# Softmax probabilities of a latent attention transposed by VectorE and DMAs through DRAM instead of TensorE, with the row sums applied to the gate

## The chip, the cores and the metric

The kernel runs on one core of one Trainium2 chip, in a single launch. The metric is the device time of the launch in microseconds. Three runs of the kernel before gave a median of 770.55 us (770.55 to 770.92).

## The reference

A trunk of two layers works on 512 tokens of width 1024, with 16 learned meta tokens ahead of them (528 tokens in all). Everything is float32. Each layer runs two token mixers on the same normalized input and adds their gated sum to the residual stream; the meta positions are dropped at the end. Cut to what matters:

```python
h = rmsnorm(h_res, norm_gain[l])
proj = h @ w_in[l]
u_pool, z_pool, c_q, c_kv, k_rope, z_mla, g_pool, g_mla = split(proj)
y_pool = (pool_mix(u_pool, ...) * silu(z_pool)) @ pool_w_up[l]
o_mla = mla(c_q, c_kv, k_rope, pos, ...)            # 8 heads, 96 wide for q and k, 64 for v
y_mla = (o_mla * silu(z_mla)) @ mla_w_up[l]
merged = sigmoid(g_pool) * y_pool + sigmoid(g_mla) * y_mla
h_res = h_res + merged @ w_out[l]
```

The attention inside `mla`, for each head, with a causal mask:

```python
s = einsum('bqhd,bkhd->bhqk', q, k) * scale
p = softmax(where(valid, s, MASK_VALUE), axis=-1)
o = einsum('bhqk,bkhd->bqhd', p, v)
```

## The kernel before

Activations lie transposed in SBUF, features on the partitions and the 528 tokens along the free dimension. Every float32 product is made of three passes of TensorE in a faster float32 format: an operand is split in a high part (a ScalarE copy) and a low part (a VectorE subtraction), and `mm3` (lines 180 to 184, the lines L181, L182 and L183 of the profile) multiplies high by high, high by low and low by high. Weights come by DMA on SP's queue into raw buffers (`fetch`, L114), and `wload` splits each 128x512 piece into `whi` (ScalarE, L176) and `wlo` (VectorE, L177), three buffers each, four pieces ahead.

The order of the program is written by hand. All weight products stand in one list `plan`; `stream` walks through it, and each `step` issues the next few matmuls and adds their planned duration (n columns at 2.4 GHz) to a clock. Attention and the norms are written as ordinary code that pulls filler from this stream: `fill_now(ns)` issues so much of it, and `gap` issues `FILL` ns but stops when the product named by `RESERVE` is done, so that later ones are left over for the end of the attention. The filler of the attention of a layer is, in this order, `pu0` to `pu7` (the end of the pooling mixer), `zm0` to `zm3`, `gp0` to `gp7` and `gm0` to `gm7` (the gates). `after(ns, fn)` issues something so much planned time later, and the tile scheduler orders the instructions of each engine by its own timeline; `follow` and `behind` add dependencies to it. Layer 1 leaves out the meta queries.

One head of the attention has these steps. `prep` scales the keys of the head (VectorE L742, GpSimd L743), splits them into `kh` and `kl`, splits the queries and copies their rotary part by SBUF-to-SBUF DMA (L756). `head` makes the scores of four blocks of 128 queries against their causal keys (272, 400, 528 and 144 columns, the 528 in two parts, L771 and L806), adds the mask and takes the row maximum on VectorE (L774), and exponentiates on ScalarE with the row sum as accumulator (L781) into the tiles `pa`, `pb` and `pc`. VectorE inverts the sums (L827), and GpSimd multiplies the probabilities by them (L834, and L832 for the 16 meta columns). `pv` of the previous head transposes the ten causal 128x128 blocks through TensorE against an identity (L859), splits each result out of PSUM into `th` and `tl` (ScalarE L275, VectorE L276), and multiplies by V: `both` (L872) takes the high part against V's high and low halves, `low` (L876) the low part against V's high half. It is cut in three parts that lie around the gaps of the next head, and some of its passes are interleaved with other matmuls (`hosts`). The 16 meta columns of two heads are collected in `pm`, transposed in four 32x128 pieces (L848), split (L903 to L905) and multiplied at once (L922). The result is multiplied by `silu(z_mla)`, which lies in `zms`.

There are four gaps a head, eight heads a layer.

Of the kernel before, what the change touches and what calls it, by code (L numbers as in the profile page):

```python
# [18 lines left out]
P = 128  # L19
DEPTH = 2  # L20
# [32 lines left out]
FILL = (2950.0, 2850.0)  # L53
RESERVE = ("gm5", "gm5")
# [3 lines left out]
WARM = 8  # L58

# [12 lines left out]
def trunk(ctx, tc, xT, xrow, mrow, pos, win, wkr, wqb, wkb, wvb, wgr, wpu, wmu, wout, gains, const, yT):  # L72
# [23 lines left out]
    def sqt():  # L96
        return tp.tile([P, HALF], F32, tag="sq", name=nm("sq"), bufs=16)
# [72 lines left out]
    def wload(src, n, spare):  # L170
        raw = early.pop(0) if early else fetch(src, n, rawt(), sp)
        loads[0] += 1
        pool, th, tl, nb = (tp, "th", "tl", 2) if loads[0] <= 2 or spare else (wp, "whi", "wlo", 3)
        hi = pool.tile([P, W if pool is tp else 512], F32R, tag=th, name=nm("whi"), bufs=nb)
        lo = pool.tile([P, W if pool is tp else 512], F32R, tag=tl, name=nm("wlo"), bufs=nb)
        act.activation(hi[:, :n], raw[:, :n], AF.Copy)  # L176
        dve.tensor_sub(lo[:, :n], raw[:, :n], hi[:, :n].bitcast(F32))  # L177
        return hi, lo
# [134 lines left out]
    kdr = [dp.tile([H, T], F32, name=f"kdr{l}") for l in range(DEPTH)]  # L313

    hbuf = [(slot(f"hh{k}", F32R), slot(f"hl{k}", F32R)) for k in range(8)]

    class Layer:
        def __init__(self, l):
# [11 lines left out]
            self.sq = []  # L330
# [147 lines left out]
        def kr_rest(self, a, b):  # L478
# [5 lines left out]
            q = sqt()  # L484
# [82 lines left out]
        def mix(self, m, s):  # L567
# [7 lines left out]
            t = "tl" if m % 2 else "th"  # L575
            self.ys[m] = (slot(f"u{m}", F32R), tp.tile([P, W], F32R, tag=t, name=nm(t), bufs=2))
# [46 lines left out]
        def ev_k(self, p):  # L623
            def ev(ps, a, b):
# [6 lines left out]
                q = self.ksq[:, a:b] if p < 3 else sqt()[:, :b - a]  # L631
# [5 lines left out]
        def v_body(self, k, w):  # L637
# [17 lines left out]
            ps = mmt()  # L655
            for k in range(2):
                r = slot("pa", F32R, bufs=2, w=416)[:, 0:4 * NM].rearrange("p (a b) -> p a b", a=4)
# [18 lines left out]
        def q_stat(self, ps, a, b, c):  # L676
            for a0, b0 in FULL:
                a0, b0 = max(a, a0), min(b, b0)
                if a0 < b0:
                    q = sqt()  # L680
                    made = act.activation(q[:, :b0 - a0], ps[:, a0 - a:b0 - a], AF.Square)
                    self.stat(q[:, :b0 - a0], a0, b0, c, made)
# [76 lines left out]
        def head(self, h, kq, prev):  # L759
# [3 lines left out]
            pa = slot("pa", bufs=2, w=416)  # L763
            pb = slot(f"cq{8 + odd}")
            pc = slot(f"cq{10 + odd}")
            bia = sm.tile([P, 5], F32, tag="bia", name=nm("bia"), bufs=2)
            rs = sm.tile([P, 5], F32, tag="rs", name=nm("rs"), bufs=2)

# [17 lines left out]
            first = scores(1, s1, 0, 272)  # L786
            if self.hosted is not None:
                follow(first, self.hosted)
            scores(3, s3, 0, SPL)
            tops = [top(1, 1, s1, causal(272)), top(3, 4, s3, maskw[:, 0:SPL])]  # L790
# [3 lines left out]
            self.tops = tops + [top(2, 2, s2, causal(400))]  # L794
# [9 lines left out]
            scores(3, s4, SPL, T)  # L804
            def passes(out, q0, n):
# [3 lines left out]
            if self.last:  # L809
                scores(0, s0, 0, 144)  # L810
            else:
                sm_ = sc[0:NM, 432:432 + NM]
                todo = passes(s0, slice(NM, NM + P), 144) + passes(sm_, slice(0, NM), NM)
                if prev is None:
                    for fn in todo:
                        fn()
                else:
                    self.pv(prev, 1, todo)
# [6 lines left out]
            expo(0, 0, s0, pt[0])  # L825
            dve.tensor_add(rs[:, 3:4], rs[:, 3:4], rs[:, 4:5])
            dve.reciprocal(rs[:, 0:4], rs[:, 0:4])  # L827
            if odd == 0:
                self.pm = sm.tile([P, 4, 32], F32, tag="pm", name=nm("pm"), bufs=2)
            for i in range(4):  # L830
                n = pt[i].shape[1]
                gp.tensor_mul(self.pm[:, i, 16 * odd:16 * odd + 16], pt[i][:, 0:NM],  # L832
                              rs[:, i:i + 1].to_broadcast([P, NM]))
# [3 lines left out]
        def pv(self, prev, part, hosts=()):  # L837
            if prev is None:
                return
            h, pt, pm = prev  # L840
            p, odd = h // 2, h % 2
            final = h == H - 1
            if part == 0:
                self.o = sct() if final else pp.tile([P, 512], F32, tag="o", name=nm("o"), bufs=1)
                if odd == 1:
                    self.turn = srows[:, 0:512].rearrange("p (c i r) -> p c i r", c=4, i=4)
                    for c in range(4):
                        ins = dve.transpose(self.turn[:, c].rearrange("p a b -> p (a b)"),  # L848
                                            pm[32 * c:32 * c + 32].rearrange("p a b -> p (a b)"))
                        if not final:  # L850
                            for t in self.tops:
                                follow(ins, t)
            ops = self.o

            def turned(js):
                tr, c = mmt(), 0
                for j in js:
                    for i in range(j, 4):
                        pe.transpose(tr[:, c:c + P], pt[i][:, NM + P * j:NM + P * (j + 1)], ident)  # L859
                        c += P  # L860
                th = tp.tile([P, W], F32R, tag="th", name=nm("th"), bufs=2)
                tl = tp.tile([P, W], F32R, tag="tl", name=nm("tl"), bufs=2)
                return th, tl, split(th, tl, tr[:, :c], 0, c)

            def ready(t, fn):
                ins = fn()
                behind(ins, t[2])
                return ins

            def both(j, t, c):  # L870
                n = SEQ - P * j
                return pe.matmul(ops[:, P * j:512], vt[:, j, h, :], t[0][:, c:c + n], start=j == 0, stop=j == 3)  # L872

            def low(j, t, c, a=0, b=512):
                a, b = max(a, P * j), min(b, 512)
                return pe.matmul(ops[0:64, a:b], vt[:, j, h, 0:64], t[1][:, c + a - P * j:c + b - P * j],  # L876
                                 start=False, stop=j == 3, skip_group_check=True)

            def chain(*fns):
                last = None  # L880
                for fn in fns:
                    ins = fn()
                    if last is not None:
                        follow(ins, last)
                    last = ins
                return last

            if part == 0:
                self.t01 = [turned((0,)), turned((1,))]
            if part == (0 if final else 1):  # L890
                t0, t1 = self.t01
                if hosts:
                    chain(lambda: both(0, t0, 0), lambda: ready(t0, hosts[0]), lambda: low(0, t0, 0, 0, 256), hosts[1],
# [323 lines left out]
```

## Time and profile before

| | |
|---|---|
| median of three runs | 770.55 us |
| span of the profiled execution (its own time is not listed apart from its span) | 768.5 us |
| TensorE, weight loads (PEld) | 763.8 us (99%), 697.9 us (91%) |
| VectorE, ScalarE, GpSimd | 544.1 us (71%), 408.9 us (53%), 201.6 us (26%) |
| DMA | 84.05 MB, 35.6% of 16 engines on SP's queue |
| L859, transposes through TensorE | 160 instructions |
| L834, L832 on GpSimd | 64 and 64 instructions |

A profile is of one execution. A busy time is the time in which at least one instruction of the engine ran; matmuls overlap, so the duration of one (mean ns) is longer than its place in the stream. In rows of groups the shapes are out<-in, then come the count, the busy time, the mean and the idle time of the engine ahead of them with what ended it. In the list of waits a row reads: engine, tile and line, what it waited for, total us, times, longest us.

### The profile page before, as it was taken

What the parts mean: (1) busy time and instruction counts of PE and PEld (TensorE: products, weight loads), DVE (VectorE), ACT (ScalarE), POOL (GpSimd) and SP (SyncE); (2) the same over time, 40 slices, a digit from 0 to 9 for tenths busy, and PEclk for the clock granted to TensorE, in tenths of its full rate; (3) what the DMA queues carried; (4) which work ended last, traced back from release to release, by engine and by line L of the source; (5) the groups of instructions that cost most, each with busy time, mean ns of one, the idle gap of its engine ahead of it and who ended that gap; (6) DMA issues with size and microseconds to landing.
All of it is one profiled execution on the core that took longest, in us unless ns stands there. A gap on an engine that the chain in (4) does not pass through costs nothing.

```text
span 768.5 us, 14355 instructions
## 1 busy us (share of the span) xinstructions
PE 763.8 (99%) x5195; PEld 697.9 (91%) x5195; DVE 544.1 (71%) x1179; ACT 408.9 (53%) x892; POOL 201.6 (26%) x251
## 2 busy tenths in 40 slices
PE   9999999999999999999999999999999999999998
PEld 9999999999999999999997898887888888888887
DVE  5588687357899977785376486773677989775842
ACT  6755656545556665634264355454446666664320
POOL 2026204012242233052220262040132434420500
PEclk9999999999999999999999999999999999999999
DMA  8533233343223222325642333334433332222372
GB/s 293 160 113 98 75 97 98 104 141 105 89 79 91 84 71 70 107 71 169 178 133 97 110 86 89 96 87 127 125 119 90 94 93 77 82 69 70 119 222 98
DMA packets 54931, 84.05 MB, mean 109 GB/s; under 512 B 10006, under 2 KB 18582, under 8 KB 54860
## 3 DMA queue, kind: packets, MB, share of 16 engines
q1 hardware_dynamic: 54716, 82.87, 35.6%
q8 instruction: 41, 0.67, 0.4%
q14 instruction: 30, 0.25, 0.1%
q10 hardware_dynamic: 144, 0.26, 0.1%
HBM read 76.69 MB, written 4.29 MB: 105 GB/s over the span
## 4 chain that ended last, share of the span: by engine, by line
PE 99%; DMA 0%; ACT 0%; DVE 0%; SPq 0%; issue 0%; ACTq 0%
PE mm L181 29%; PE mm L183 29%; PE mm L182 29%; PE mm L859 2%; PE S L181 2%; PE S L182 2%; PE S L183 2%; PE o L876 1%; PE o L872 1%; PE S L503 1%; PE S L470 0%; DMA xb<-xT 0%; PE S L806 0%; PE mm L922 0%; PE mm L395 0%; PE S L872 0%
## 5 line engine op out<-in xcount | busy, mean ns | idle before, releaser
L181 PE MATMUL mm<-hh,whi 128*128 128x264 f32 (+2 forms) x1080 | 339.9, 317 | 0.0
L182 PE MATMUL mm<-hl,whi 128*128 128x264 f32 (+2 forms) x1080 | 338.2, 314 | 0.0
L183 PE MATMUL mm<-hh,wlo 128*128 128x264 f32 (+2 forms) x1080 | 337.1, 315 | 0.0
L177 DVE TENSOR_TENSOR wlo<-raw,whi 128x512 fp32r<-128x512 f32 (+2 forms) x251 | 186.7, 748 | 98.6 <-ACT whi L176 94.6
L176 ACT ACTIVATE whi<-raw 128x512 fp32r<-128x512 f32 (+2 forms) x251 | 150.2, 602 | 181.3 <-PE mm L182 135.3
L181 PEld LDWEIGHTS mm<-hh,whi 128*128 128x128 f32 x1080 | 202.5, 188 | 12.9 <-ACT kp L474 0.4
L182 PEld LDWEIGHTS mm<-hl,whi 128*128 128x128 f32 x1080 | 203.0, 188 | 12.2
L183 PEld LDWEIGHTS mm<-hh,wlo 128*128 128x128 f32 x1080 | 201.9, 188 | 12.2
L743 POOL TENSOR_TENSOR tmp<-kp,bc 64x528 f32<-64x528 f32 x16 | 25.6, 1600 | 123.9 <-PE mm L183 70.0
L604 POOL TENSOR_TENSOR racc<-racc,tmp 128x264 f32<-128x264 f32 (+1 forms) x15 | 14.3, 956 | 133.1 <-ACT tmp L603 133.1
L832 POOL TENSOR_TENSOR pm<-pa,rs 128x16 f32<-128x16 f32 x32 | 9.1, 285 | 126.1 <-DVE rs L827 126.1
L982 POOL TENSOR_TENSOR tmp<-tmp,xb 128x264 f32<-128x264 f32 (+1 forms) x24 | 26.9, 1138 | 56.0 <-DVE tmp L980 55.9
L774 DVE CUSTOM_DVE_ANT_0 S<-S,maskw,nqs 128x400 f32<-128x400 f32 (+4 forms) x80 | 38.4, 499 | 4.4 <-PE S L183 4.0
L781 ACT ACTIVATE cq<-S,bia 128x400 f32<-128x400 f32 (+2 forms) x48 | 24.6, 516 | 27.1 <-DVE bia L774 18.1
L181 PE MATMUL mm<-u,whi 128*128 128x264 f32 (+1 forms) x108 | 34.7, 322 | 0.0
L181 PE MATMUL mm<-cq,whi 128*128 128x264 f32 (+1 forms) x108 | 34.7, 321 | 0.0
L183 PE MATMUL mm<-u,wlo 128*128 128x264 f32 (+1 forms) x108 | 34.7, 321 | 0.0
L183 PE MATMUL mm<-cq,wlo 128*128 128x264 f32 (+1 forms) x108 | 34.5, 321 | 0.0
L182 PE MATMUL mm<-cq,whi 128*128 128x264 f32 (+1 forms) x108 | 34.5, 321 | 0.0
L834 POOL TENSOR_TENSOR cq<-cq,rs 128x384 f32<-128x384 f32 (+1 forms) x32 | 32.8, 1024 | 0.0
L276 DVE TENSOR_TENSOR tl<-mm,th 128x384 fp32r<-128x384 f32 (+1 forms) x48 | 27.9, 596 | 5.0 <-ACT th L275 4.8
L275 ACT ACTIVATE th<-mm 128x384 fp32r<-128x384 f32 (+1 forms) x48 | 24.1, 523 | 10.2 <-PE mm L859 9.2
(270 smaller groups left out, 1378.6 us busy)
## 6 DMA issues: line engine op xcount, KB each, us to landing
raw<-win SPq DMA_DIRECT2D x143, 256.0 KB, 2.6
raw<-wout SPq DMA_DIRECT2D x32, 256.0 KB, 3.0
bc<-kdr SPq DMA_DIRECT2D x16, 264.0 KB, 3.6
raw<-wpu SPq DMA_DIRECT2D x16, 256.0 KB, 2.7
raw<-wmu SPq DMA_DIRECT2D x16, 256.0 KB, 2.7
raw<-wqb SPq DMA_DIRECT2D x12, 256.0 KB, 2.6
xb<-xT SPq DMA_DIRECT2D x8, 264.0 KB, 5.7
tmp<-xT SPq DMA_DIRECT2D x16, 132.0 KB, 3.4
```

Of the source, the lines that this page charges most:

```text
L176: act.activation(hi[:, :n], raw[:, :n], AF.Copy)
L177: dve.tensor_sub(lo[:, :n], raw[:, :n], hi[:, :n].bitcast(F32))
L181: first = pe.matmul(out, wh, xh, start=start, stop=False)
L182: pe.matmul(out, wh, xl, start=False, stop=False)
L183: newest[0] = pe.matmul(out, wl, xh, start=False, stop=stop)
L275: act.activation(hi[:, a:b], src, AF.Copy)
L276: return dve.tensor_sub(lo[:, a:b], src, hi[:, a:b].bitcast(F32))
L743: gp.tensor_mul(kf[r0:r0 + 64, :], self.kp[r0:r0 + 64, :], bc[r0:r0 + 64, :])]
L774: return dve.tensor_tensor_reduce(out=sv, in0=sv, in1=mask, scale=nqs[:, i, h:h + 1], scalar=3e38, op0=ALU.add, op1=ALU.min, accum_out=bia ...
L781: act.activation(pv, sv, AF.Exp, scale=-1.0, bias=bia[:, i:i + 1], accum_out=rs[:, c:c + 1])
L834: gp.tensor_mul(pt[i][:, NM:], pt[i][:, NM:], rs[:, i:i + 1].to_broadcast([P, n - NM]))
L982: gp.tensor_add(t[:, :b - a], t[:, :b - a], self.am[m][:, a:b])
```

## The change

The transposes through TensorE are dropped. When a query block has been exponentiated, the new function `turn` copies its 16 meta columns (GpSimd) and lets VectorE transpose its causal 128x128 blocks in 32x32 pieces into one tile D of ten blocks. After the last block, SP issues four DMAs, one for each 32 partitions, that write D to a DRAM buffer with the 32x32 pieces at their transposed places, and GpSimd issues one DMA that reads it back into a tile E. In the next head, `parts` splits E into high (a `wide` tile) and low (in place), in two pieces of 640 columns, and `pv` multiplies, now in one piece, its moving operand read in runs of 32 columns out of that layout. The probabilities are no longer multiplied by the inverted row sums. Instead these are written to DRAM, read back spread over 64 partitions by a DMA that GpSimd issues, and multiplied into `zms` on GpSimd, once for two heads. The meta columns are transposed in one piece, split, written to DRAM and read back by three DMAs (`meta_turn`).

The fillers shrink, the reserve grows, tile D has one buffer and E two, the second buffers of `pa`, `pb` and `pc` go, and the squares for the norms move from tiles of their own into parts of `xb`, D and E (`halves`). `th` and `tl` become halves of one wide tile.

```diff
-FILL = (2950.0, 2850.0)
-RESERVE = ("gm5", "gm5")
+FILL = (2620.0, 2530.0)
+RESERVE = ("gm3", "gm3")
+NB = 10
+def block(i, j):
+    return 2 * i + j if j < 2 else 1 if i == 2 else 6 + j
...
+    def att(tag):
+        return sl.tile([P, NB * P], F32 if tag == "D" else F32R, tag=f"att{tag}", name=nm(f"att{tag}"), bufs=1 if tag == "D" else 2)
...
+            def turn(i):
+                gp.tensor_copy(pm[:, i, 16 * odd:16 * odd + 16], pt[i][:, 0:NM])
+                for j, n in ((0, i + 1),) if i in (0, 1, 3) else ((0, 2), (2, 1)):
+                    k = block(i, j)
+                    dve.transpose(grid[:, :, k:k + n, :].rearrange("p b s r -> p s b r"), pt[i][:, NM + P * j:NM + P * (j + n)])
...
             expo(1, 1, s1, pt[1])
             expo(2, 2, s2, pt[2])
+            turn(1)
+            turn(2)
             self.gap()
-            self.pv(prev, 0)
-            if self.last:
-                self.pv(prev, 1)
+            self.parts(prev)
             self.gap()
...
             expo(0, 0, s0, pt[0])
+            turn(3)
+            turn(0)
             dve.tensor_add(rs[:, 3:4], rs[:, 3:4], rs[:, 4:5])
             dve.reciprocal(rs[:, 0:4], rs[:, 0:4])
-            for i in range(4):
-                n = pt[i].shape[1]
-                gp.tensor_mul(self.pm[:, i, 16 * odd:16 * odd + 16], pt[i][:, 0:NM],
-                              rs[:, i:i + 1].to_broadcast([P, NM]))
-                gp.tensor_mul(pt[i][:, NM:], pt[i][:, NM:], rs[:, i:i + 1].to_broadcast([P, n - NM]))
-            return h, pt, self.pm
+            row = rdr[self.l][h]
+            sp.dma_start(row.rearrange("a (p i) -> p (a i)", i=4), rs[:, 0:4])
+            got = att("E")
+            n = NB * 32
+            via = pdr[h % 2]
+            for a in range(4):
+                sp.dma_start(via[:, n * a:n * a + n].rearrange("(b k) x -> k b x", k=32),
+                             blocks[32 * a:32 * a + 32, :].rearrange("p (b x) -> p b x", x=n))
+            gp.dma_start(got.bitcast(F32), via)
+            gp.dma_start(rb[64 * odd:64 * odd + 64, 0:512], row.partition_broadcast(64))
+            if odd == 1:
+                self.meta_turn(pm)
+                z = self.zms[h // 2][:, NM:T].rearrange("p (i q) -> p i q", i=4)
+                gp.tensor_mul(z, z, rb[:, 0:512].rearrange("p (q i) -> p i q", i=4))
+            return h, got
...
+        def parts(self, prev):
+            h, got = prev
+            hi = wide()
+            f = got.bitcast(F32)
+            for a in (0, NB * 64):
+                split(hi, got, f[:, a:a + NB * 64], a, a + NB * 64)
+            self.pt = hi, got
...
-            def turned(js):
-                tr, c = mmt(), 0
-                for j in js:
-                    for i in range(j, 4):
-                        pe.transpose(tr[:, c:c + P], pt[i][:, NM + P * j:NM + P * (j + 1)], ident)
...
+            for j in range(4):
+                k0, n = block(j, j), 4 - j
+                st = block(j + 1, j) - k0 if n > 1 else 1
+                hi, lo = (t.rearrange("p (a s r) -> p s a r", a=4, s=NB)[:, k0:k0 + st * (n - 1) + 1:st] for t in self.pt)
+                chain(pe.matmul(o[:, P * j:512], vt[:, j, h, :], hi, start=j == 0, stop=j == 3))
...
+                chain(pe.matmul(o[0:64, P * j:512], vt[:, j, h, 0:64], lo, start=False, stop=j == 3, skip_group_check=True))
...
             for h in range(H):
-                kn_ = self.head(h, kq, prev)
+                now = self.head(h, kq, prev)
                 self.gap()
                 if h + 1 < H:
                     kq = self.prep(h + 1)
-                self.pv(prev, 2)
-                prev = kn_
+                self.pv(prev)
+                prev = now
                 self.gap()
...
+            self.parts(prev)
+            fill_now(2600)
+            self.pv(prev)
```

More of the change, by code (lines that the diff above doesn't have):

```diff
@@ L630, in ev @@
                     self.ksq = slot("bc", bufs=3)
[L631 removed]
+                q = self.ksq[:, a:b] if p < 3 else next(self.half)[:, :b - a]
                 made = act.activation(q, k, AF.Square)
@@ L879, in chain @@
[L879 to L893, printed above, removed]
-                          lambda: low(0, t0, 0, 256, 512))
-                    self.hosted = chain(lambda: both(1, t1, 0), lambda: ready(t1, hosts[2]), *hosts[3:], lambda: low(1, t1, 0))
-                else:
-                    for j, t in enumerate(self.t01):
-                        both(j, t, 0)
-                        low(j, t, 0)
```

156 lines of the change are left out of this document (75 added, 81 removed).

## The prediction

> **What bounds the kernel now.** I read the page first, then the waits of TensorE, then all waits, then the busy time by stretches.
>
> ```profile
> span 768.5 us, 14355 instructions
> PE 763.8 (99%) x5195; PEld 697.9 (91%) x5195; DVE 544.1 (71%) x1179; ACT 408.9 (53%) x892; POOL 201.6 (26%) x251
> PE 99%; DMA 0%; ACT 0%; DVE 0%; SPq 0%; issue 0%; ACTq 0%
> ```
> ```profile
> PE wps L136 <- DVE na L715: 1.1, 1, 1.1
> PE S L181 <- ACT hh L340: 0.3, 1, 0.3
> ```
> TensorE is busy for 99% of the span, the chain that ended last is TensorE's from end to end, and its list of waits has two entries, 1.4 us together. So a matmul that is taken away is time gained, one for one, as long as nothing else becomes late. Other engines wait for TensorE's progress instead:
>
> ```profile
> ACT whi L176 <- PE mm L182: 135.3, 103, 3.9
> ```
> ```profile
> SPq L114 <- DVE wlo L177: 375.5, 170, 7.9
> ```
> ScalarE stands 135.3 us because the weight buffers are still full, and SP 375.5 us because the raw buffers are: weights are ahead of their use. That is the cover on which the rest draws. Which engine comes next is read in the attention stretches (the first three rows are layer 0, the last is layer 1):
>
> ```profile
> core 0: us, PE busy (x) PEld busy (x) DVE busy (x) ACT busy (x) POOL busy (x), PEclk, DMA share, GB/s
> 185.00:219.00 34.00, 34.00 (x285) 33.92 (x284) 27.85 (x69) 19.31 (x50) 10.66 (x15) 1.00 0.28 87
> 219.00:270.00 51.00, 51.00 (x425) 50.78 (x425) 48.05 (x114) 32.03 (x78) 16.85 (x27) 1.00 0.27 82
> 270.00:304.00 34.00, 34.00 (x285) 33.85 (x284) 25.72 (x67) 19.89 (x52) 9.68 (x17) 1.00 0.23 71
> ...
> 606.00:657.00 51.00, 51.00 (x270) 43.08 (x269) 45.74 (x102) 31.84 (x73) 23.19 (x31) 1.00 0.28 82
> ```
> VectorE is the runner-up: 82%, 94%, 76%, and 90%. In the second row the gp products are the filler, which cost VectorE most. The granted clock is 1.00 in each. These windows hold two, three, two and three heads, 17 us each (worked out below).
>
> **TensorE: what goes.** Per head, ten 128x128 transposes through TensorE are dropped (L859).
>
> ```profile
> L859 PE MATMUL mm<-cst,cq 128*128 128x128 f32 x112 | 20.4, 272 | 0.0
> ...
> L859 PE MATMUL mm<-cst,pa 128*128 128x128 f32 x48 | 10.3, 272 | 0.0
> ```
> ```profile
> 207.11 0.77 PE mm L859 x7
> ...
> 328.29 0.49 PE mm L181 x4
> ```
> The 272 ns are latency, and overlap. On the chain seven take 0.77 us, so 0.11 us each; 112 + 48 = 160 of them are 17.6 us. That is the term of the gain. The products with V keep their columns: per head 1280 for the high and 1280 for the low part. A 264-column matmul takes 0.49 / 4 = 0.1225 us on the chain, 0.46 ns a column, so these are 2560 x 0.46 = 1.2 us a head. (A head is 17 us: its scores, 1360 columns in three passes, 1.9; this 1.2; the transposes 1.1; and four fillers of 2.95 planned us. A planned 264 columns is 264 / 2.4 = 110 ns against 122.5 here, so these are 13.1.) What changes in them is the pattern: the moving operand is now read in runs of 32 elements (128 bytes) out of rows of 1280. No row here reads a moving operand so. Bounds: nothing, or each column twice, which is 16 x 1.2 = 18.8 us and the whole gain. I take nothing, since the nearest rows, 264 columns read in one run, are paced by columns, and a run of 32 is long beside one element. The Trainium skill, "SBUF — State Buffer" (section "SBUF: two separate sides"), says that accesses in the same 16-byte line go at full rate; four of ours share each line, and by that the term is nothing too, which no run here shows. Seven second halves of the split low products of layer 0 go as well; their columns stay, so I put them at nothing.
>
> **VectorE: what is exchanged.** Per head it transposes 1280 columns in 32x32 blocks (512, 256, 256, 128, 128), and splits the returned probabilities in two pieces of 640 instead of three out of PSUM (512, 384, 384).
>
> ```profile
> L712 DVE STREAM_TRANSPOSE tmp<-srows x2: 678/680/681, 151.8 to 537.4; 32x512 f32<-32x512 f32 x2
> ```
> ```profile
> L177 DVE TENSOR_TENSOR wlo<-raw,whi 128x512 fp32r<-128x512 f32 x33 | 25.8, 783 | 8.1 <-ACT whi L176 7.9
> L619 DVE SCALAR_TENSOR_TENSOR xb<-tmp,xb 128x264 f32<-128x264 f32 x16 | 9.2, 573 | 0.8 <-ACT tmp L618 0.8
> L276 DVE TENSOR_TENSOR tl<-mm,th 128x384 fp32r<-128x384 f32 x14 | 7.7, 551 | 0.5 <-ACT th L275 0.4
> L617 DVE TENSOR_TENSOR tmp<-mm,rinv 128x264 f32<-128x264 f32 x16 | 6.7, 425 | 0.2
> ...
> L276 DVE TENSOR_TENSOR tl<-mm,th 128x512 fp32r<-128x512 f32 x7 | 4.8, 687 | 1.2 <-ACT th L275 1.0
> L848 DVE STREAM_TRANSPOSE srows<-pm 32x128 f32<-32x128 f32 x16 | 4.8, 299 | 0.3
> ...
> L904 DVE TENSOR_TENSOR racc<-srows,racc 32x512 fp32r<-32x512 f32 x3 | 2.0, 682 | 0.5 <-ACT racc L903 0.4
> ```
> Transposes: 0.68 + 2 x 0.43 + 2 x 0.30 = 2.1 us (0.43 lies a third of the way from 299 to 680 ns). Splits: 0.69 + 2 x 0.55 = 1.8 us go, and two of 640, extended from 551 and 687 to 0.82 each, come: -0.15. Per pair of heads four transposes of 299 and one L904 of 682 ns go, one transpose and one short subtraction of about 0.3 each come: -1.3, or -0.65 a head. Net +1.3 us a head.
>
> Two things come off. The filler between heads falls from 4 x 2.95 to 4 x 2.62 planned us, so 1.45 real us of filler leave each head. A gp product of 5.9 us costs VectorE 2 x 0.69 + 2 x 0.43 + 2 x 0.43 = 3.1 us, so about 0.75 go. And GpSimd's multiplications by the row sums (L832, L834) go:
>
> ```profile
> 246.88 0.43 DVE L617 TENSOR_TENSOR tmp<-mm,rinv 128x264 f32<-128x264 f32 x1
> 247.22 1.71 DVE L177 TENSOR_TENSOR wlo<-raw,whi 128x512 fp32r<-128x512 f32 x1
> ```
> ```profile
> 247.04 1.34 POOL L743 TENSOR_TENSOR tmp<-kp,bc 64x528 f32<-64x528 f32 x1 [5.31 <-DVE xb L619]
> ```
> A subtraction that starts while GpSimd multiplies takes 1.71 us against 0.69 of its size alone; in the mean L177 takes 783, and L619 573 against 425 for the same 264 columns. Half of that excess, 0.4 us a head, I give to the multiplications that go; L743 stays. The Trainium skill, in the same section of that page, calls the shared port an exclusive lock between a VectorE instruction with two SBUF inputs and a GpSimd one; the trace agrees (1.71 us). By that rule all of the excess outside L743 goes, up to 0.8, and VectorE's sum below would be 0.4 lower.
>
> So a head in the gp stretch asks 16.0 + 1.3 - 0.75 - 0.4 = 16.15 us of VectorE, and TensorE gives it 17 - 1.1 - 1.45 = 14.45. That is over 100%. Over the four heads that gp then covers (eight products of 48 x 0.110, 42 planned us, at 10.5 a head) 4 x 1.7 = 6.8 us are short in layer 0; in layer 1, from 15.25, 4 x 0.95 = 3.8. Together 10.6 us. Against it: the stretches of zm and gm have room (14.1 and 13.0 of 14.45 by the same sum), and the filler kept back for the end grows from two gm products to four, some 23 us. VectorE can fall behind in gp and catch up there, since the order within an engine's queue is not the order of the source:
>
> ```profile
> 215.92 2.08 POOL L743 TENSOR_TENSOR tmp<-kp,bc 64x528 f32<-64x528 f32 x1 [12.21 <-DVE xb L619]
> 219.46 0.25 POOL L832 TENSOR_TENSOR pm<-pa,rs 128x16 f32<-128x16 f32 x1 [1.46 <-DVE rs L827]
> ```
> L743 here prepares head 3 and runs ahead of head 2's L832, though the source issues it later. I take about half of the shortage, 5 us, as lost on TensorE.
>
> **The trip through DRAM.** Each head writes 640 KB in four DMAs on SP's queue and reads them back in one on GpSimd's. From the last score matmul of a head to its row sums:
>
> ```profile
> 231.22 0.13 PE S L806 x4
> ```
> ```profile
> 237.50 0.18 DVE L827 RECIPROCAL rs<-rs 128x4 f32<-128x4 f32 x1 [0.20 <-ACT pa L781]
> ```
> ```profile
> raw<-win SPq DMA_DIRECT2D x143, 256.0 KB, 2.6
> ...
> bc<-kdr SPq DMA_DIRECT2D x16, 264.0 KB, 3.6
> ...
> scr<-xb SPq DMA_DIRECT2D x8, 132.0 KB, 3.2
> ...
> nq<-nsr SPq DMA_DIRECT2D x2, 8.2 KB, 1.7
> ```
> ```profile
> L756 SPq DMA_DIRECT2D qhl<-q x32: 507/540/1247, 126.8 to 647.7; - x32
> ```
> It is 6.3 us to the sums; the transposes behind them 1.0; four issues of 0.54, 2.2; the write, as 132 KB into DRAM, 3.2; the read between 2.6 (256 KB at its price) and 9.0 (2.5 times 264 KB at 3.6), I take 5, the middle, as one DMA pays its start once. GpSimd issues no DMA in this trace; from 0.5 (SP's) to 1.3 (its own L743), I take 1. Then ScalarE and VectorE split, a copy ahead of two subtractions of 0.82, 2.3. Sum 21 us, from 18 to 25. The Trainium skill, "DMA: Bandwidth & Descriptors" (section "Anatomy of one DMA"), gives 2.0 us and the bytes at 436 GB/s, an estimate of 3.5 each way; the sum would be 20, and no run here shows such a DMA.
>
> In the source, five gaps, the scores of the next head and one product with V lie between (13.1 planned, 14.6 real, + 3.1): 17.7 us. The trip is 3 us longer. It is not a loop: a head's product may slide behind more filler, and at the end of a layer the four gm products give 23 us and the gaps before them more. So in the sum it costs nothing if the queues' order allows for it, and it is the rival if not. Queued behind its waits: on SP, behind the four writes, the weight loads, whose cover is the 375.5 us above; on GpSimd, behind the read, L743 for the next head; on VectorE, behind the next head's first transposes, which need the one buffer D free of the writes, the weights' subtractions.
>
> The rest is hidden. The z multiplication and the copies run on GpSimd, at 26%; ScalarE's pieces keep their size; the traffic adds 1.31 MB a head, 91 GB/s on 82 at a DMA share of 0.27, so some 0.57.
>
> **The sum.** On the profiled span of 768.5, less 17.6, plus 5: 756. The timed runs have a median of 770.55, 2.05 above the span, so about 758. Less than 0.2% (1.5 us) this kernel's measurement would hardly tell from no change.
>
> **Rivals.**
> *VectorE becomes the bound.* If nothing is caught up, all 10.6 come back: 770.55 - 17.6 + 10.6 = 764. For it: 94% and 90%. Against it: TensorE did not wait once at 94%, and the reserve. Chance 0.09.
> *The trip arrives late where a queue waits for it, and the kernel is slower.* ScalarE's copy of the returned probabilities, or GpSimd's read, stands at the head of its queue while weights, L743 and PSUM wait behind it. It decides from 17.6 / 16 = 1.1 us a head that reach TensorE; the trip is 3 us past its written place, and its bounds reach 7. With 2 us a head, 32 in all, 770.55 - 17.6 + 32 = 785. For it: DRAM and GpSimd's issue are not in the trace, and a VectorE without spare time can't make up a stand. Against it: the reordering shown, and weights ahead by buffers. Chance 0.36.
> *The reads wait for VectorE.* GpSimd writes what a DMA it issues needs, and collides with VectorE as L743 does: 1.0 us (1.71 less 0.69) on each of 16 reads, 16 us if none is covered: 769. The Trainium skill, "SBUF — State Buffer" (section "SBUF: two separate sides"), warns of that for DMAs issued by GpSimd beside VectorE instructions that use both ports. The instructions of the attention windows read PSUM or two tensors, or transpose. Chance 0.03.
> *The strided reads count double:* 770.55 - 17.6 + 18.8 = 772, no gain; the change does not do what it says. Chance 0.02.
>
> **How the numbers follow.** The forecast, 758 with its own range 752 to 764 (17.6 and a little, to 6.5), has 0.50. Faster: 0.50 + 0.09 = 0.59. Within 0.2%: 0.05, the last two rivals. Slower: 0.36. The range starts at 752 and goes into the late trip up to 788, leaving some 0.15 above and 0.03 below.
>
> **What the profile would show.** No L859 and TensorE's busy sum near 747; 40 new VectorE transposes a layer of 0.30 to 0.68 us, and a few for the meta tokens; VectorE near 100% in the gp windows; TensorE's waits few. I am wrong if TensorE's waits name the returned probabilities, or ScalarE a DMA into them, with over 17 us; if the matmuls with V take more than 0.46 ns a column; or if VectorE's share stays under 90% and TensorE still waits.

## The result: 808.06 us against 770.73, and the profile after

The changed kernel takes 808.06 us (median of four runs, 802.79 to 808.25), the kernel before 770.73 beside it (770.45 to 770.80 beside the experiments below). The ratio is 1.046 (1.043 to 1.049): 37 us are lost where 12.5 were forecast to be gained. The page of the changed kernel, its span, its engines and its chain:

```profile
span 806.5 us, 14299 instructions
...
PE 767.0 (95%) x5028; PEld 694.1 (86%) x5028; DVE 556.2 (69%) x1219; ACT 398.2 (49%) x868; POOL 198.2 (25%) x251
...
PE 45%; DMA 12%; DVE 5%; issue 2%; ACT 2%; SPq 1%; POOL 0%; POOLq 0%; DVEq 0%; ACTq 0%
```
TensorE has 167 instructions fewer, and yet is busy for longer (767.0 against 763.8 us) and idle for 39.5 us where it was 4.7. The chain that ended last was TensorE's alone; now 12% of it are DMAs. TensorE's own waits, and those of the other engines that bear on them (engine, tile and line, what it waited for, total us, times, longest):

```profile
PE o L918 <- ACT th L295: 21.7, 9, 4.5
PE S L918 <- ACT th L295: 5.4, 2, 3.8
```
```profile
ACT th L295 <- DMA attE<-pdr: 64.5, 16, 8.9
...
DVE attE L296 <- ACT th L295: 45.2, 15, 6.5
POOL attE L870 <- DMA pdr<-attD: 40.8, 6, 8.5
...
POOL u L875 <- DMA cq<-rdr: 21.4, 8, 4.3
...
POOL cq L871 <- DMA rdr<-rs: 17.7, 6, 6.4
```
L918 and L921 are the products with V, high and low; L295 and L296 the ScalarE copy and the VectorE subtraction that split the returned probabilities; L870 the large read on GpSimd, L871 the read of the row sums, L875 the product of the gate. The first row of the second list is the one that the prediction named as its refutation: ScalarE stands 64.5 us, once for each of the 16 heads, for the returned probabilities. VectorE stands behind it, and TensorE behind both.

One head, the first of layer 1, shows how. Its trip on the chain (start, duration, what; L841 is its last score, L868 are the four writes on SP), then TensorE, and then all engines in the next head, where TensorE's stand is longer (columns as in the windows of before):

```profile
586.17 0.19 PE S L841 x2
...
592.31 0.34 SPq L868
...
594.33 4.07 DMA pdr<-attD
...
598.51 0.68 issue
599.20 5.35 DMA attE<-pdr
...
604.57 0.74 ACT th L295
...
605.34 0.69 DVE attE L296
...
606.52 0.74 DVE attE L296
```
```profile
622.74 0.39 PE L202 MATMUL mm<-hl,whi 128*128 128x512 f32 x1
622.97 0.39 PE L203 MATMUL mm<-hh,wlo 128*128 128x512 f32 x1
626.82 0.80 PE L918 MATMUL o<-th,vt 128*128 128x512 f32 x1 [3.47 <-ACT th L295]
627.41 0.63 PE L201 MATMUL mm<-hh,whi 128*128 128x512 f32 x1
627.84 0.63 PE L202 MATMUL mm<-hl,whi 128*128 128x512 f32 x1
628.26 0.63 PE L203 MATMUL mm<-hh,wlo 128*128 128x512 f32 x1
630.13 0.69 PE L921 MATMUL o<-attE,vt 128*64 128x512 f32 x1 [1.23 <-DVE attE L296]
```
```profile
620.00:625.00 5.00, 3.35 (x15) 2.38 (x13) 0.00 (x0) 0.00 (x0) 2.49 (x5) 1.00 1.00 302
625.00:630.00 5.00, 2.08 (x4) 1.16 (x4) 3.83 (x3) 3.56 (x8) 3.99 (x3) 0.64 0.02 6
```
From 620 to 625 ScalarE and VectorE do nothing at all: ScalarE has the copy of the returned tile at the head of its queue, VectorE what follows it, and behind these stand the splits of the next weights. TensorE has the product with V at the head of its own queue: it waits 3.47 us for the copy itself and 1.23 us for VectorE's part of the split. The three passes between the two (L201 to L203) had their weights already and stood behind the product. Of the 36.1 us in TensorE's list of waits 28.3 are at L918 and L921, and 5.3 are for split weights. Then TensorE pays a second time. A 512-column matmul went every 0.23 us (622.74 to 622.97); after the stand it takes 0.43 (627.41 to 627.84), and the granted clock is 0.64 in that stretch. The Trainium skill, "TensorE: Matmul & The Clock Gate" (section "Part 1: The HAM clock gate (the "warmup" mystery)"), says that an idle window of some 3.4 us halves the clock; the trace agrees only in part. After each of the five stands of 3.0 us and more (4.50, 3.16, 3.01, 3.76 and 3.47) the granted clock is 0.50 for 3.4 or 6.8 us, though two of them are shorter than 3.4. After 1.08 us (605.99) the spacing stays at 0.23. In between it goes both ways: after stands of 2.39 us (234.86) and 2.44 (310.38) the clock stays at 1.00, after another of 2.39 (683.35) and after 1.42 and 0.80 close together (648.34 and 649.64) it falls to 0.50.

### The profile page after: what moved, and what is told of

Its sections match the earlier page's. It is cut to its first block, busy times and chain, and to the rows that moved or that the text cites. A ratio compares the mean times of both kernels' runs of the same rounds, so it can differ in the third digit from the quotient of the medians.

```text
span 806.5 us, 14299 instructions
## 1 busy us (share of the span) xinstructions
PE 767.0 (95%) x5028; PEld 694.1 (86%) x5028; DVE 556.2 (69%) x1219; ACT 398.2 (49%) x868; POOL 198.2 (25%) x251
## 4 chain that ended last, share of the span: by engine, by line
PE 45%; DMA 12%; DVE 5%; issue 2%; ACT 2%; SPq 1%; POOL 0%; POOLq 0%; DVEq 0%; ACTq 0%
PE mm L203 14%; PE mm L202 14%; PE mm L201 14%; DMA attE<-pdr 8%; DMA pdr<-attD 3%; DVE attE L296 2%; ACT th L295 1%; DVE attD L816 1%; SPq L868 1%; DVE wlo L197 1%; DMA mdr<-cq 1%; PE S L201 1%; PE S L203 1%; PE S L202 1%; DMA rdr<-rs 1%
## 5 line engine op out<-in xcount | busy, mean ns | idle before, releaser
L203 PE MATMUL mm<-hh,wlo 128*128 128x264 f32 (+2 forms) x1072 | 339.2, 319 | 4.5 <-DVE wlo L197 4.5
L201 PE MATMUL mm<-hh,whi 128*128 128x264 f32 (+2 forms) x1072 | 339.9, 319 | 0.8 <-ACT whi L196 0.8
L197 DVE TENSOR_TENSOR wlo<-raw,whi 128x512 fp32r<-128x512 f32 (+2 forms) x242 | 173.3, 719 | 90.7 <-ACT whi L196 87.3
L196 ACT ACTIVATE whi<-raw 128x512 fp32r<-128x512 f32 (+2 forms) x242 | 144.6, 600 | 159.6 <-PE mm L202 130.6
L203 PEld LDWEIGHTS mm<-hh,wlo 128*128 128x128 f32 x1072 | 204.1, 191 | 18.5 <-DVE wlo L197 6.1
L201 PEld LDWEIGHTS mm<-hh,whi 128*128 128x128 f32 x1072 | 204.5, 191 | 14.4 <-ACT whi L196 1.1
L296 DVE TENSOR_TENSOR attE<-attE,th 128x640 fp32r<-128x640 f32 x32 | 33.7, 1072 | 45.2 <-ACT th L295 45.2
L295 ACT ACTIVATE th<-attE 128x640 fp32r<-128x640 f32 x32 | 21.8, 729 | 64.5 <-DMA attE<-pdr 64.5
L918 PE MATMUL o<-th,vt 128*128 128x512 f32 (+3 forms) x56 | 19.8, 362 | 21.7 <-ACT th L295 21.7
L803 DVE CUSTOM_DVE_ANT_0 S<-S,maskw,nqs 128x288 f32<-128x288 f32 (+4 forms) x80 | 37.3, 494 | 4.3 <-PE S L203 3.8
L201 PE MATMUL mm<-cq,whi 128*128 128x264 f32 (+1 forms) x108 | 34.8, 322 | 0.0
L202 PE MATMUL mm<-th,whi 128*128 128x264 f32 (+1 forms) x108 | 34.6, 321 | 0.0
L201 PE MATMUL mm<-u,whi 128*128 128x264 f32 (+1 forms) x108 | 34.6, 320 | 0.0
L203 PE MATMUL mm<-cq,wlo 128*128 128x264 f32 (+1 forms) x108 | 34.5, 321 | 0.0
L203 PE MATMUL mm<-u,wlo 128*128 128x264 f32 (+1 forms) x108 | 34.5, 319 | 0.0
L918 PEld LDWEIGHTS o<-th,vt 128*128 128x128 f32 x56 | 12.0, 214 | 26.0 <-ACT th L295 24.7
```

Of the source, the lines that this page charges most:

```text
L201: first = pe.matmul(out, wh, xh, start=start, stop=False)
L202: pe.matmul(out, wh, xl, start=False, stop=False)
L203: newest[0] = pe.matmul(out, wl, xh, start=False, stop=stop)
L295: act.activation(hi[:, a:b], src, AF.Copy)
L296: return dve.tensor_sub(lo[:, a:b], src, hi[:, a:b].bitcast(F32))
L803: return dve.tensor_tensor_reduce(out=sv, in0=sv, in1=mask, scale=nqs[:, i, h:h + 1], scalar=3e38, op0=ALU.add, op1=ALU.min, accum_out=bia ...
```

## The experiments

Two theories were set against each other. The first: the trip of the probabilities arrives late at queues that stand for it (place and order). The second: its price, whoever waits, that is VectorE's extra work, GpSimd's part, or the tighter packing of the filler.

**e5_fill: only the new filler and reserve, on the kernel before.**

```diff
-FILL = (2950.0, 2850.0)
-RESERVE = ("gm5", "gm5")
+FILL = (2620.0, 2530.0)
+RESERVE = ("gm3", "gm3")
```


> The kernel before with the smaller fillers and the larger reserve of the kernel after alone; nothing is left out. The filler is only moved behind the attention, so late trip and VectorE alike expect the time of the kernel before within 0.5%: 768 to 774. If it is 780 or more, part of the loss is the packing of the heads and not the trip.

Measured: 771.25 us, ratio 1.000 (0.999 to 1.001). On the kernel before, the packing costs nothing by itself.

**e4_sp: SP issues the large read in place of GpSimd.**

```diff
-            gp.dma_start(got.bitcast(F32), via)
+            sp.dma_start(got.bitcast(F32), via)
```


> The kernel after with the one large read of each head issued by SP instead of GpSimd; nothing is left out. GpSimd's issue as the cost: the read starts 1 us or more earlier in each head, 16 us or more less, 792 or below. Late trip: the issue is 0.6 us of a trip of 20 us, so the read alone gains under 0.5 us a head, but SP's queue now stands for the writes with weight loads behind it, so 800 to 825.

Measured: 807.73 us, ratio 1.048 (1.046 to 1.050), as the changed kernel, within the 800 to 825 that the late trip asked for. Among the waits stands

```profile
ACT th L295 <- DMA attE<-pdr: 60.8, 16, 7.1
```
So neither GpSimd's issue nor its place in GpSimd's queue is what makes the probabilities late.

**e1_stale: the large read takes a buffer that no head writes.** The DMA, its bytes and all engine work stay; the wait for the head's own writes goes.

```diff
-            gp.dma_start(got.bitcast(F32), via)
+            gp.dma_start(got.bitcast(F32), stale)
```


> The kernel after, but each head's read from DRAM takes a buffer that no head writes (filled once with weights), so that the read waits for no write; the writes, the bytes, VectorE's work and the strided reads stay. It leaves out the true probabilities. Late trip (ScalarE's copy stands in its queue for the read, 64.5 us in the kernel after, TensorE idles and its granted clock falls): ScalarE's waits for the read fall under 5 us, TensorE's clock is 1.00, and the time is 752 to 758. VectorE as the bound: VectorE's work is the same, so TensorE still waits by 10 us or more, 764 or above. Strided moving operand: 770 or above with TensorE busy to the end.

Measured: 776.57 us, ratio 1.007 (1.006 to 1.009): 31.5 us come back, but not all that was expected (752 to 758). The waits show what took over:

```profile
POOL cq L875 <- DMA rdr<-rs: 96.5, 14, 9.5
...
ACT th L295 <- DMA attE<-stale: 20.5, 9, 5.0
...
PE mm L937 <- DMA racc<-mdr: 7.0, 2, 3.8
```
GpSimd now stands 96.5 us for the row sums on their way into DRAM (the read of them is L875 here), the read of the next probabilities is issued behind that, and TensorE waits for the meta columns. The prediction had not priced these small trips at all. In the changed kernel their DMAs last as long as the large ones (issue to landing, the last column, in us):

```profile
pdr<-attD SPq DMA_DIRECT2D x64, 160.0 KB, 3.1
attE<-pdr POOLq DMA_DIRECT2D x16, 640.0 KB, 5.8
...
cq<-rdr POOLq DMA_DIRECT2D x16, 128.0 KB, 5.6
...
rdr<-rs SPq DMA_DIRECT2D x16, 2.0 KB, 3.8
```
The row sums, 2 KB, take 3.8 + 5.6 = 9.4 us out and back; the probabilities, 640 KB, take 3.1 + 5.8 = 8.9 behind the issue of their last write. The 5.6 is not the price of the small read by itself. In eleven of the 16 heads GpSimd issues it right behind the large read, and it lands behind that; issued apart from it, as in e1, it takes 3.0 in the median (2.7 to 4.8).

**e7_small: only the small reads from that buffer; e6_nosmall: the small and the large ones.** e7 has these two edits, e6 has them and e1's.

```diff
-            gp.dma_start(rb[64 * odd:64 * odd + 64, 0:512], row.partition_broadcast(64))
+            gp.dma_start(rb[64 * odd:64 * odd + 64, 0:512], stale[h:h + 1, 0:512].partition_broadcast(64))
...
-                             via[:, P * c:P * c + P].rearrange("(a r) x -> r a x", a=4))
+                             stale[:, P * c:P * c + P].rearrange("(a r) x -> r a x", a=4))
```


> The kernel of the first experiment (the large read waits for no write), and the two small reads through DRAM, of the row sums and of the meta columns, wait for no write either; all writes, all bytes and all VectorE work stay. It leaves out the true probabilities, row sums and meta columns. Small trips (the 6 us that the first experiment still lies above the kernel before, and its 23 above the sum, come from GpSimd's queue: the gate multiplication waits there for its read, with the next head's keys and reads behind it): GpSimd's waits for DMAs nearly vanish and the time is 752 to 758. VectorE as the bound: 765 to 776, with TensorE waiting for VectorE's weights.

> The changed kernel, with only the small trips (row sums and meta columns) read from a buffer that no head writes; the probabilities take their real trip. This leaves the row sums and the meta columns of each head out of the result. Theory (the trip of the probabilities is the larger cause by itself, and ScalarE's copy stands for it at 64 us): 795 to 804, a few us better than 807. Rival (the two kinds of trips only add up: 14.6 us come off): 790 to 795. Second rival (the small trips in GpSimd's in-order queue carry the large one along with them, so most of the loss goes): under 780.

Measured: e6 761.94 us, ratio 0.989 (0.987 to 0.990); e7 790.91 us, ratio 1.026 (1.024 to 1.027). With the two kernels above this is a square:

| us | probabilities make their trip | from the other buffer |
|---|---|---|
| small trips real | 808.06 | 776.57 |
| small trips from the other buffer | 790.91 | 761.94 |

The probabilities' trip costs 31.5 us beside the real small trips and 29.0 without them; the small ones 17.2 and 14.6. They nearly add up, so each is a cause of its own. That is the first rival of e7's expectation (790 to 795); its theory was too high, and e6 lies 4 us above the 752 to 758 expected of it. In e7 the large trip still holds TensorE:

```profile
PE o L922 <- ACT th L295: 16.7, 8, 5.1
PE S L922 <- ACT th L295: 4.6, 2, 3.4
```
In e6 TensorE waits 5.0 us in all, 3.4 of them once, for ScalarE's split of the keys. Without waits for a trip, then, the same instructions and the same DMA traffic are 8.5 us faster than the kernel before.

**e2_later: the split and the products with V half a head later.** The split is also tied to the newest filler matmul, so that it can't move ahead in ScalarE's and VectorE's queues.

```diff
-            self.parts(prev)
+            self.pv(self.ready)
...
-                self.pv(prev)
-                prev = now
+                self.parts(prev)
+                self.ready = prev
+                prev = now
...
-                split(hi, got, f[:, a:a + NB * 64], a, a + NB * 64)
+                behind(act.activation(hi[:, a:a + NB * 64], f[:, a:a + NB * 64], AF.Copy), newest[0])
+                dve.tensor_sub(got[:, a:a + NB * 64], f[:, a:a + NB * 64], hi[:, a:a + NB * 64].bitcast(F32))
...
```
The diff leaves out the end of the attention, which gets one filler and one product more, and the last step of a pair of heads (`part2`), which follows after one `LAG` instead of two in all pairs but the last.

> The kernel after with the split of the returned probabilities moved from the first gap of the next head to its end, tied behind the newest filler matmul issued there, and the product with V moved into the first gap of the head after; nothing is left out. That is about 6.7 us later for ScalarE's copy, against a mean stand of 4.0 us and a longest of 8.9. Late trip: ScalarE's waits for the read fall from 64.5 us to under 20, TensorE's idle time from 39.5 to under 12, and the time to 755 to 775. VectorE as the bound: no change in what VectorE does, so still over 790.

Measured: 782.74 us, ratio 1.016 (1.011 to 1.021). That is outside the 755 to 775 expected, though the direction is that of the first theory and the time is below VectorE's 790. ScalarE's stand falls from 64.5 to 28.5 us (under 20 was expected) and TensorE's idle time from 39.5 to 21.7 (under 12). GpSimd's small trips are what is late next:

```profile
POOL cq L871 <- DMA rdr<-rs: 49.9, 10, 7.5
...
ACT th L897 <- DMA attE<-pdr: 28.5, 11, 4.7
```

**w1: the whole pipeline one step longer.** Everything is computed. The reads of all three trips are issued in the next head's first gap, behind a filler matmul; the gate is multiplied at that head's end; the split and the products with V come in the head after.

```diff
         def head(self, h, kq, prev):
...
-            turn(1)
-            turn(2)
             self.gap()
-            self.parts(prev)
+            turn(1)
+            turn(2)
+            self.parts(self.ready)
+            fresh = self.reads(prev)
             self.gap()
+            self.pv(self.ready)
+            self.ready = fresh
...
-                self.pv(prev)
+                self.gate(self.ready)
...
```
The diff leaves out the new functions `reads` and `gate`, which hold the reads from DRAM and the gate's product, the dependencies of both and of the split on the newest filler matmul, and the end of the attention.

> The kernel after with the whole pipeline one step longer, nothing left out: all reads from DRAM are issued by GpSimd in the first gap of the next head, tied behind the newest filler matmul, the gate multiplication at the end of that head, the split in the first gap of the head after that, the product with V in its second gap, and the first two blocks' transposes after the first gap. Late trips: every queue then meets data that has landed, ScalarE's waits for the read fall under 10 us, TensorE's clock stays 1.00, and the time is 753 to 765, below the kernel before. VectorE as the bound: over 768.

Measured: 757.83 us, ratio 0.983 (0.981 to 0.985). It beats the changed kernel by 50 us and the kernel before by 12.6. The page, and what is left of ScalarE's wait:

```profile
PE 751.6 (99%) x5028; PEld 685.0 (91%) x5028; DVE 553.5 (73%) x1219; ACT 399.0 (53%) x868; POOL 196.7 (26%) x251
```
```profile
ACT th L912 <- DMA attE<-pdr: 0.8, 1, 0.8
```
The trips are no shorter (large read 5.6 us, its writes 3.0); ScalarE, VectorE and TensorE no longer stand for them. Four waits of 1.8 us in all are TensorE's list.

**w2_nolow: w1 without VectorE's subtraction of the returned probabilities.** Is the rest over 770.45 - 17.6 = 753 us VectorE's shortage?

```diff
-                dve.tensor_sub(got[:, a:a + NB * 64], f[:, a:a + NB * 64], hi[:, a:a + NB * 64].bitcast(F32))
```


> The pipeline that is a step longer, with VectorE's subtraction of the returned probabilities left out: the low operand of the products with V is the returned tile itself, so that part of the computation is changed. TensorE's work and all DMAs are as they were. VectorE loses 16 pairs of subtractions of some 0.8 to 1.07 us, about 1.9 us a head, 30 us in all, of which the four heads of each gp stretch hold 8. Theory (VectorE is the bound of the gp stretches, and the last 5 us over 753 are its shortage): 752 to 754. Rival (the rest has another cause, such as weight loads or the packing of the filler): 757 to 759, no change.

Measured: 758.38 us, ratio 0.984 (0.982 to 0.985). No change, though VectorE is busy for 19 us less. The stretches of the gp products, w1 first:

```profile
219.00:270.00 51.00, 50.83 (x405) 49.47 (x405) 48.50 (x127) 32.55 (x80) 14.94 (x25) 1.00 0.69 182
606.00:657.00 51.00, 51.00 (x250) 42.63 (x249) 50.66 (x116) 32.51 (x76) 19.87 (x31) 1.00 0.74 186
```
```profile
219.00:270.00 51.00, 50.65 (x402) 49.08 (x401) 46.01 (x122) 33.29 (x81) 15.83 (x30) 1.00 0.69 185
606.00:657.00 51.00, 50.49 (x248) 41.90 (x247) 49.07 (x110) 31.02 (x72) 19.21 (x30) 1.00 0.72 184
```
VectorE at 95% and 99% does not hold TensorE up.

**w5_fill and w6_fill: w1 with a longer and a shorter filler.**

```diff
-FILL = (2620.0, 2530.0)
+FILL = (2750.0, 2650.0)        # w5; w6: (2500.0, 2410.0)
```


> The pipeline that is a step longer, with longer fillers (2750 and 2650 planned ns) and the same reserve. VectorE has 0.6 us more room a head in the gp stretches. If VectorE is the bound there: 755 to 757. Rival (no bound of VectorE): 757 to 759.

> The pipeline that is a step longer, with shorter fillers (2500 and 2410 instead of 2620 and 2530 planned ns) and the same reserve, so that more filler is kept back for the end of the attention. If VectorE is the bound of the gp stretches the same work asks the same of VectorE per gp product, but fewer products stand beside a head: a head then asks 15.9 of VectorE and TensorE gives 14.0, which is worse in the gp heads, but gp then covers a little more of the heads: within 2 us of 757.8 either way. Rival (the trips need the time): slower by 3 us or more.

Measured: w5 764.08 us, ratio 0.991 (0.989 to 0.993); w6 772.52, ratio 1.003 (1.001 to 1.004). Both lose, by 6 and by 15 us. For w6 the time is the rival's, for w5 it is neither theory's. The traces show where the time goes, not why. w6's profiled span is 17.5 us longer than w1's (774.0 against 756.5): TensorE waits 12.3 us where it waited 1.8, and is busy for 758.5 against 751.6, with a granted clock of 0.991. A head is 4 x 0.12 = 0.5 planned us shorter, and waits for the split are back in TensorE's list, this one first:

```profile
PE o L934 <- ACT th L912: 3.3, 3, 1.3
```
With 1.1 us for VectorE's part of the split these are 4.4 of the 12.3; the others are for keys, weights and the like. So it is not shown that the trips make the loss. In w5 TensorE waits 5.9 us, and 3.1 of what is added are for VectorE (its part of the split, 1.8, and weights, 1.3). More room for VectorE did not make the kernel faster, but VectorE is not cleared of a part in this loss, and why w5 loses was not tried. w1's filler is a narrow place.

## Why the prediction was wrong, step by step

**The step that failed** is the last of the trip through DRAM: "So in the sum it costs nothing if the queues' order allows for it, and it is the rival if not." The 3 us of lateness that it let pass were counted at the wrong place. A trip of 21 us, to the end of the split, was held against the place of the product in TensorE's stream, 17.7 us behind the last score. In the first head of layer 1, shown above, both are about right: from the last score matmul (586.2) to the end of the split (607.3) it is 21.1 us, and TensorE comes to the product after 18.7 us and waits 1.08. But the first reader of the tile is ScalarE's copy, and `parts` stands two gaps ahead of `pv` in the source. By the prediction's own rates three gaps, the next head's first scores (912 columns in three passes) and one product lie ahead of it, 8.8 + 1.3 + 1.2, some 11 us, and the data land after 21 less 2.3 for the split, 18.7. At this place the trip is 7 us late. The trace has it so: ScalarE comes to the copy at 596.7, 10.5 us behind the last score, and stands 7.88 us.

**"It is not a loop"** failed with it. These are the next head's last score, ScalarE at the copy, its first exponential behind it, and the next head's writes:

```profile
599.26 0.27 PE L841 MATMUL S<-kh,qhl 128*128 128x144 f32 x1
```
```profile
604.57 1.36 ACT L295 ACTIVATE th<-attE 128x640 fp32r<-128x640 f32 x2 [7.88 <-DMA attE<-pdr]
605.84 0.57 ACT L810 ACTIVATE cq<-S,bia 128x400 f32<-128x400 f32 x1
```
```profile
612.62 2.53 SPq L868 DMA_DIRECT2D pdr<-attD  x4
```
The exponentials of the next head wait behind the copy of this one, so its first write is issued 13.4 us after its last score, where this head took 6.1, and its own trip takes 30.8 us. In the first head of each layer the trip takes 19.0 and 21.1 us; in the other 14 it takes 22.5 to 32.4, and 27.6 in the mean of all 16. Its part through DRAM is as estimated: from the first write's issue to ScalarE's start 11.9 us in the mean, for 2.2 + 3.2 + 1 + 5 = 11.4 (5 was called the middle of 2.6 and 9.0, which is 5.8). What grew is the way from the last score to the first write: 12.2 us in the mean for 6.3 + 1.0. Not all of that is the stand: in w1, where ScalarE hardly stands, this way is still 8.4 us.

The rival that came true was priced at 785 (2 us a head, 32 in all, chance 0.36). In kind and in size its stands were right: ScalarE stands 64.5 us, 4 us a head, and TensorE's idle time grows by 34.8. That the time is not 785 but 808, outside the range too, comes from TensorE's busy time, which no part of the prediction let grow.

**Two terms were missing.** The small trips, in the square above 15 to 17 us; the prediction counted the z multiplication and the copies as "hidden" on an engine at 26%, but not the waits ahead of them in that engine's queue. And the clock, which is halved after each stand of 3 us or more and after some shorter ones. In the changed kernel the mean granted clock is 0.979; 2.1% of 806.5 are an estimated 17 us of full-speed time that TensorE was not given, some of it while it was idle. TensorE's busy time (767.0) exceeds what was forecast (763.8 less 17.6, 746.2) by 20.8 us. w1, at a clock of 1.000, is busy for 751.6, so 5.4 of these have another cause, and 15.4 are left for the clock.

**The sum, closed.** The span grew by 38.0 us: 17.6 gone with the transposes, 34.8 more idle time on TensorE (39.5 less 4.7), and 20.8 more busy time. These 55.6 us against the ideal are, by the runs, 31.5 for the trip of the probabilities (808.06 less 776.57), 14.6 for the small trips (776.57 less 761.94), and some 9 that are left in e6 (761.94 less 753): there TensorE is idle for 8.1 us against 4.7, and busy for 752.2 against 746.2. That most of the clock's 15 us lie within the first two, and are not to be added, is seen in e6 and w1, where the clock is 0.995 and 1.000.

**TensorE: what goes.** No transposes are left, and the gain is real: w1 takes 12.6 of the 17.6 us. The remaining 5 us were not settled. They are not waits: w1's idle time is 4.9 us against 4.7 before, and its busy time is the 5.4 us above the forecast. Part is read from the chains. The attention of layer 0 runs from its first score matmul to the statistics of the next layer; before, then w1:

```profile
171.23 0.31 PE S L181 x2
...
410.34 1.03 PE mm L395 x16
```
```profile
172.87 0.30 PE S L201 x2
...
406.77 1.03 PE mm L418 x16
```
239.1 against 233.9 us: 5.2 of the 8.8 us that its 80 transposes are worth. And w1 came to that attention 1.6 us later, which w2 did not (171.39). Of the 12.0 us between the two spans that leaves 8.4 for what follows, of 8.8 that layer 1's transposes are worth. What takes 3.6 us in layer 0 is open; VectorE's subtraction of the probabilities it is not (w2 takes 233.8 for the same stretch).

**The strided operand** was taken as free, and is. Products with V where the clock is 1.00, before (240 to 300 us) and after (280 to 300 us; count, busy, mean ns):

```profile
L872 PE MATMUL o<-th,vt 128*128 128x512 f32 x4 | 1.6, 391 | 0.0
```
```profile
L918 PE MATMUL o<-th,vt 128*128 128x512 f32 x1 | 0.4, 397 | 0.0
```
397 against 391 ns for 512 columns. These are durations; from start to start, seven products of 2048 columns in all pass in 0.95 us there (296.84 to 297.79), 0.46 ns a column, as the prediction had it. The rival of the double read is out.

**VectorE.** The transposes cost what was extended from other rows (0.68 and 0.43 us were given):

```profile
L816 DVE STREAM_TRANSPOSE attD<-cq 128x512 f32<-128x512 f32 x16 | 11.2, 700 | 0.2
...
L816 DVE STREAM_TRANSPOSE attD<-pa 128x256 f32<-128x256 f32 x16 | 6.7, 421 | 5.8 <-DMA pdr<-attD 5.8
```
So did the split in 25 of its 32 pieces, 0.81 to 0.83 us for 0.82. Seven take 1.36 to 2.20 us and bring the mean to 1072 ns; in e6 it is 812. Of the two rows, the changed kernel's comes first:

```profile
L296 DVE TENSOR_TENSOR attE<-attE,th 128x640 fp32r<-128x640 f32 x32 | 33.7, 1072 | 45.2 <-ACT th L295 45.2
```
```profile
L296 DVE TENSOR_TENSOR attE<-attE,th 128x640 fp32r<-128x640 f32 x32 | 25.3, 812 | 4.1 <-ACT th L295 4.1
```
In the second head above the subtraction that starts at 626.17 takes 2.05 us and the one at 628.14 takes 1.93, while GpSimd multiplies the gate (1.53 us from 626.01) and the next keys (1.88 from 627.51): what is released together runs together. All seven long ones have GpSimd at work beside them, but so have some of the short ones. That this is the cause was not tried by itself. The 5 us charged for VectorE's shortage were too much: at 99% it did not hold TensorE in w1, and relief did not help. The forecast of 758 and w1's 757.83 agree by luck: 5 us that VectorE did not cost and 5 us that are open stand in each other's place. That the bound passes to VectorE (764) is seen in no run here; w5 takes 764.08, but of what its waits add only 3.1 us name VectorE.

**The reads wait for VectorE.** With the large read issued by SP, e4 is as slow, so the 16 us of this rival are not in that read. The small reads stayed with GpSimd in every run.

## What to carry to other kernels

A trip through DRAM that is a few microseconds later than the place of its first reader holds up all that queues behind that reader, on every engine that waits in order, can make the next trip late in turn, and then costs the clock. Ask for each landing which queue has its reader at the head, hold the trip against that reader's place and not against that of the product that needs it in the end, and give the reader a place that is late by a margin, tied down so that it can't move ahead. A small read that is issued behind a large one lands behind it, so a small trip needs its own place in the sum. To find what an async chain costs, let its reads take data that is ready: here that split 46 us into two causes with four kernels.

## What was not expected of the hardware

- The read of the row sums takes 5.6 us in the median, about as long as that of 640 KB (5.8), where it is mostly issued right behind it; issued apart, in e1, it takes 3.0.
- A stand of 3.47 us on TensorE is followed by 512-column matmuls 0.43 us apart in place of 0.23, until about 633; one of 1.08 us is not. Two stands of 3.01 and 3.16 us halve the clock as well, and of two of 2.39 us one does and one does not.
- A filler that is 0.12 or 0.13 us shorter or longer in each gap moved w1 by 15 and 6 us, more than the change's whole gain at one end.
